# Attention's branch of a hybrid SSD and forgetting-attention layer: low pieces of T1 and T4 made with the differences and loaded, and T3's product in a bank of its own

## The chip, the cores and the metric

The kernel runs on one core of one Trainium2 chip. The metric is the device time of one execution in microseconds; of several runs the median is given. A profile shows one execution, instruction by instruction. Its span goes from the first to the last recorded instruction, and a little time lies around it.

## The reference

One layer of a hybrid decoder, 1024 tokens by 1024 channels, float32. Two branches start from the same normalised projection, and a gated merge, an output projection and a residual follow. Cut to what matters here:

```python
h = rmsnorm(x, pre_g)
z_ssm, xbc, dt, q, k, v, f, z_att, g_ssm, g_att = split(h @ w_in)
y_ssm = group_norm(ssd(conv(xbc), dt, a) * silu(z_ssm))          # Mamba-2 branch
s     = q @ k.T / 8 + F[t] - F[s]                                # 16 heads of 64, causal, F = cumsum(log sigmoid(f))
y_att = (softmax(s) @ v) * silu(z_att)                           # attention's branch
merged = sigmoid(g_ssm) * (y_ssm @ w_branch_ssm) + sigmoid(g_att) * (y_att @ w_branch_att)
x = x + rmsnorm(merged @ w_out, post_g)
```

## The kernel before, in words

**Large products.** Every projection is done with a Strassen-Winograd scheme over 2 x 2 blocks. A `Pair` (L320) takes two groups of 128 weight columns and gives two units of 128 output channels by 1024 tokens, in halves of 512 tokens. It needs seven products instead of eight. Each has a weight side (blocks a11, a12, a21, a22 or sums of them) and a data side, an operand made of four blocks of 128 rows by 512 columns (j = 0 to 3). The map `OPERAND` (L150) names the data side of each product: 1 uses b11, 2 b21, 6 -T2, 5 T1, 7 T3, 4 T4 and 3 -b22. The differences are T1 = b12 - b11, T2 = b22 - T1, T3 = T2 - b11 and T4 = T2 - b21 (`LESS`, L167).

**Three passes.** A float32 product is made of three passes in TensorE's fp32r form: each number is split into a high piece h (rounded by a ScalarE copy) and a low piece l (VectorE: the number less h), and the passes are h*h, h*l and l*h. So one product is 4 x 3 = 12 matmuls of 128 x 128 by 512 columns (`matmuls`, L386). The operand tiles in the profile are x0 (b11), x1 (b21), x2 (-b22), x3 (T1), x4 (-T2), x5 (T3) and x6 (T4), with h or l behind the number; a pair's split weights are `wop`.

**Where a product goes.** Products 1, 6, 7 and 4 of a pair add to one PSUM bank (`self.b`, shown as pb). After 1, 6 and 7 the running sum is copied to SBUF by ScalarE (`keep`, L399, line L402 of the profile), and TensorE can add the next product only after that copy. Products 5 and 3 add in another bank (pc). `give` (L405) forms a result from a bank and a kept sum on VectorE (L415 to L419), and the result of product 4 on ScalarE (L413), with the sign turned.

**The order.** `Stream` (L461) writes the order of all products by hand, pair after pair, two halves of six matmuls each. `half` (L535) issues one half, prepares the weights of the product three steps on (`prepare`: split on ScalarE L349 and VectorE L350, sums L355 on VectorE or GpSimd), fetches and splits operands of the next branch (`some`, L294), and runs one waiting chore from the list `chores`. The pairs after the projections are four of the Mamba branch (`ends[0:4]`, operands `ops_s`), four of attention's branch (`ends[4:8]`, operands `ops_a`) and four of the output projection (`ends[8:]`, operands `ops_w`). The first of attention's four, called a in the constructor, runs its products in the order 1, 5, 6 and then, when attention is done, 7, then product 1 of the next pair b, and 2, 4, 3.

**Attention** (L1327 to L1733) goes over eight head pairs hp and six groups g of query blocks each. One step m = 6 hp + g issues scores (L1476: TensorE, then VectorE's row maximum L1505 and ScalarE's exponential L1509), the weighted values of the step before (L1552), some halves of the stream, the transposes of the exponentials (L1511, L131) with their copies (L1546, L1548), and again some halves. Most instructions that belong to a step are pinned (`pin`): on each engine they keep the order of the program. TensorE's are all pinned. Unpinned instructions are placed by the framework when it builds the program.

**Differences of attention's branch.** A head pair hp gives block k = hp of y_att. For hp below 4 (L1580) the block's T1 is formed on VectorE from the outputs (`first`, L1585) and stored to DRAM by a chore through GpSimd's queue (`store`, L192, L193 of the profile). For hp = 4 to 6 `second` (L1592) makes T2 and T3, and `last` (L1607, L1609) makes T4, block j = hp - 4; they are stored likewise. For hp = 7 all are made in place and split without DRAM (`put`, L287, and `direct`, L282). `fetch` (L257) loads a block, raw, into the low tile, on SyncE's queue (SP, L263), and `split` (L265) makes its high piece on ScalarE (L275 or L278) and its low piece on VectorE (L276 or L279). For `ops_w` there is another way already: blocks named in `lows` have had their low piece made early and stored, so `fetch` loads both pieces (the raw block into the high tile) and `split` only rounds the high one.

**Small buffers.** `small` (L136) gives a tile of 128 x 512 floats from one pool of four buffers with the tag th. Gates and results of the stream (th), the fetched blocks of the differences (y, and th at L206), the softmax sums on their way (st, L1431, and rb, L1438) all take them. An instruction that fills a new one waits until the old one's last reader is done, which can be a store's landing.

Of the kernel before, what the change touches and what calls it, by code (L numbers as in the profile page):

```python
# [12 lines left out]
ALU = mybir.AluOpType  # L13
# [73 lines left out]
def hybrid_layer(ctx: ExitStack, tc, a, out):  # L87
# [71 lines left out]
    class Operands:  # L159
# [9 lines left out]
        def __init__(self, name, src, there=lambda k, h: True, order=lambda op: op, queue=nc.gpsimd):  # L169
            self.src, self.there, self.order, self.queue = src, there, order, queue  # L170
            self.copy = src
            self.tiles, self.left, self.made, self.at, self.step = {}, {}, set(), {}, 0
            self.lows = {}
            self.dram = {n: tc.dram_tile([KH, P, HALF], F32, name=f"{n}_{name}") for n in self.LESS}

        def __getitem__(self, name):
# [7 lines left out]
            return self.dram[name][j]  # L184

        def ready(self, name, j):
            if name in self.BLOCKS:
                r, h = self.BLOCKS[name]
                return self.there(KH * r + j, h)
            return (name, j) in self.made  # L190

        def store(self, name, j, t, cols=slice(0, HALF)):  # L192
            pin(self.queue.dma_start(self.dram[name][j][:, cols], t))  # L193
            if cols.stop == HALF:
                self.made.add((name, j))

        def differences(self, j, x, other, cols=slice(0, HALF), room=2, third=None):

# [65 lines left out]

        def split(self, name, j, raw=None):  # L265
            h, l = (t[:, j, :] for t in self.tiles[name])
            if name.strip("-") in self.lows:

                pin(nc.scalar.activation(h, h.bitcast(F32), AF.Copy, scale=-1.0 if name[0] == "-" else 1.0))
                self.left[name].remove(j)  # L270
                return
            if raw is None:
                raw = l.bitcast(F32)
            if name[0] == "-":
                pin(nc.scalar.activation(h, raw, AF.Copy, scale=-1.0))  # L275
                pin(nc.vector.scalar_tensor_tensor(l, raw, -1.0, h, ALU.mult, ALU.subtract))  # L276
            else:
                pin(nc.scalar.activation(h, raw, AF.Copy))  # L278
                pin(nc.vector.tensor_tensor(l, raw, h, ALU.subtract))  # L279
            self.left[name].remove(j)  # L280
# [39 lines left out]
    class Pair:  # L320
# [7 lines left out]
        def __init__(self, keys, handlers, ops=None, adds=nc.vector):  # L328
            self.keys, self.handlers = keys, handlers
            self.ops = xop if ops is None else ops  # L330
            self.adds = adds
            self.raw, self.op, self.prepared = {}, {}, set()
            self.s1, self.sums = None, 0

        def load(self, names):
            for n in names:
# [59 lines left out]
                        stop=k == KH - 1 and n == 2, skip_group_check=True,  # L396
                    )

        def keep(self, ps):  # L399
            s = wp.tile([P, HALF], F32, tag="s", bufs=3, name="s")  # L400
            with tc.high_priority():
                nc.scalar.activation(s, ps, AF.Copy)  # L402
            return s

        def give(self, unit, ch, ps, s=None, how=None):  # L405
            dst, post = self.handlers[unit][0:2]
            if s is None and hasattr(post, "direct"):
                post.direct(ch, ps)
                return
            d = dst(ch)  # L410
            with tc.high_priority():
                if s is None:
                    nc.scalar.activation(d, ps, AF.Copy, scale=-1.0)  # L413
                elif how == "sum":
                    nc.vector.tensor_tensor(d, ps, s, ALU.add)  # L415
                elif how == "less":
                    nc.vector.tensor_tensor(d, ps, s, ALU.subtract)
                else:
                    nc.vector.tensor_tensor(d, s, ps, ALU.subtract)  # L419
            post(ch)  # L420

        def begin(self, which, sums, early):
# [6 lines left out]
        def do(self, which):  # L429
            self.begin(which, self.sums, False)  # L430
            if which == 1:
                pool, tag = self.bank
                self.b = pool.tile([P, HALF], F32, tag=tag, bufs=1, name="pb")
                yield from self.matmuls(self.b, 1, "b11", True)
                self.k1 = self.keep(self.b)
            elif which == 2:
                pool, tag = self.other
                ps = pool.tile([P, HALF], F32, tag=tag, bufs=1, name="p" + tag)
                yield from self.matmuls(ps, 2, "b21", True)
                self.give(0, 0, ps, self.k1, "sum")  # L440
            elif which == 6:
                yield from self.matmuls(self.b, 6, "-t2", False)
                self.k2 = self.keep(self.b)
            elif which in (5, 7):
                if which == 5:
                    self.c = pj.tile([P, HALF], F32, tag="c", bufs=1, name="pc")
                    yield from self.matmuls(self.c, 5, "t1", True)
                else:
                    yield from self.matmuls(self.b, 7, "t3", False)
                    self.k7 = self.keep(self.b)  # L450
                self.sums += 1
                if self.sums == 2:
                    self.give(1, 1, self.c, self.k7, "less")
            elif which == 4:
                yield from self.matmuls(self.b, 4, "t4", False)
                self.give(1, 0, self.b)
            elif which == 3:
                yield from self.matmuls(self.c, 3, "-b22", False)
                self.give(0, 1, self.c, self.k2, "from")

    class Stream:  # L461
# [6 lines left out]
        def __init__(self, pairs, double, last):  # L468
            self.pairs = pairs
            for n, p in enumerate(pairs):  # L470
                p.bank, p.other = (pj, "be"[n % 2]), (pjx, "d") if n < double else (pj, "c")

                p.between = n < double or n >= last

# [6 lines left out]
                self.steps += [(p, 4), (p, 3)] if n + 1 < last else [(p, 3), (p, 4)]  # L481

            a, b, c, d, e, f, g, h = pairs[last:]
            self.steps += [(a, 5), (a, 6), (a, 7), (b, 1), (a, 2), (a, 4), (a, 3)]
            for p, nxt in ((b, c), (c, d), (d, e)):
                self.steps += [(p, 2), (p, 6), (p, 5), (p, 7), (nxt, 1), (p, 4), (p, 3)]
# [840 lines left out]
    with tc.tile_pool(name="att", bufs=1, reuse_waits="tile", side="right") as ap, tc.tile_pool(  # L1327
# [247 lines left out]
        def outputs(hp, h, zr):  # L1575
# [4 lines left out]
            if hp < KH:  # L1580
                if h == 0:
                    y = fetched("b12", hp)

                    def first():
                        pin(nc.vector.tensor_tensor(y, y, zr, ALU.subtract))  # L1585
# [207 lines left out]
```

## Time and profile before

| | us |
|---|---|
| median of 3 runs | 1278.0 (1276.09 to 1281.77) |
| the profiled execution | 1273.87 |
| its span | 1272.2 |
| TensorE busy (share of the span) | 1246.1 (98%) |
| VectorE busy | 1012.9 (80%) |
| ScalarE busy | 794.3 (62%) |
| GpSimd busy | 319.3 (25%) |
| granted TensorE clock, mean | 0.999 |

In the profile PE is TensorE's matmuls, PEld its weight loads, DVE VectorE, ACT ScalarE, POOL GpSimd and SP SyncE; SPq, ACTq and the like are instructions that only issue a DMA. A row of the timeline gives the start and the duration in us, the engine and the line of the kernel, the operation, output <- inputs, shape and count, and in brackets the idle time before it with what ended that. A matmul's record is longer than the step to the next one, since matmuls overlap. Attention's stage goes from about 670 to 1120 us; the rest of attention's branch and the output projection follow.

### The profile page before, as it was taken

The page shows a single profiled execution, that of the slowest core. Times are in us where ns is not written, and L with a number is a line of the kernel's source. Part 1 is how long each engine was busy: PE and PEld are TensorE (multiplying, and loading weights), DVE is VectorE, ACT ScalarE, POOL GpSimd, SP SyncE. Part 2 cuts the span into 40 slices and gives each one's busy share as a digit, 9 for nine tenths or more (in the row PEclk, how much of TensorE's full clock was granted, in tenths as well). Part 3 has the DMA queues.
Part 4 walks back from the last instruction along what each step waited for, and adds up shares of the span by engine and source line. Part 5 has one row for each costly group of instructions (what it writes and reads, how often), then busy time and mean ns, then how long its engine had stood idle before and what let it go on. Part 6 is the DMA issues. An engine that isn't in the chain of part 4 may idle for free.

```text
span 1272.2 us, 20822 instructions
## 1 busy us (share of the span) xinstructions
PE 1246.1 (98%) x6926; PEld 982.3 (77%) x6926; DVE 1012.9 (80%) x1994; ACT 794.3 (62%) x1737; POOL 319.3 (25%) x322
## 2 busy tenths in 40 slices
PE   5999999999999999999999999999999999999997
PEld 3678888888888888888887777777777777778886
DVE  7988886988888978997767676767789767886975
ACT  7745665556665765566555666666687666844753
POOL 4000440013400241115102124223112212356062
PEclk9999999999999999999999999999999999999999
DMA  8232452545436533744447576666687657766933
GB/s 300 69 120 76 146 162 88 191 152 182 138 101 215 175 127 117 219 146 140 142 149 252 162 228 212 217 214 218 232 286 263 224 184 249 249 221 199 364 110 105
DMA packets 152236, 233.56 MB, mean 184 GB/s; under 512 B 15201, under 2 KB 60737, under 8 KB 152129
## 3 DMA queue, kind: packets, MB, share of 16 engines
q1 hardware_dynamic: 136064, 196.08, 47.7%
q10 hardware_dynamic: 10560, 18.06, 3.8%
q0 software_dynamic: 5504, 18.09, 3.7%
q8 instruction: 54, 0.88, 0.3%
q14 instruction: 54, 0.43, 0.1%
HBM read 162.99 MB, written 72.34 MB: 185 GB/s over the span
## 4 chain that ended last, share of the span: by engine, by line
PE 86%; DMA 4%; DVE 4%; ACT 4%; issue 1%; SPq 0%; POOL 0%; DVEq 0%; ACTq 0%; POOLq 0%
PE pb L128 36%; PE pc L128 21%; PE pd L128 7%; PE av L128 5%; PE pt L131 5%; PE s L128 5%; PE yps L128 2%; PE st L128 1%; ACT ex L1509 1%; DMA xt<-in_x 1%; PE tr L131 1%; PE tr_v L131 1%; DMA v<-v_dram 1%; PE df L128 1%; DVE wop L350 1%
## 5 line engine op out<-in xcount | busy, mean ns | idle before, releaser
L350 DVE TENSOR_TENSOR wop<-sum,wop 128x512 fp32r<-128x512 f32 x180 | 140.2, 780 | 53.6 <-ACT wop L349 52.6
L349 ACT ACTIVATE wop<-sum 128x512 fp32r<-128x512 f32 x180 | 112.5, 626 | 109.0 <-DVE sum L355 52.4
L1509 ACT ACTIVATE ex<-ex,nm 128x512 f32<-128x512 f32 (+1 forms) x192 | 116.2, 606 | 71.9 <-DVE nm L1505 71.6
L402 ACT ACTIVATE s<-pb 128x512 f32<-128x512 f32 x144 | 85.3, 593 | 98.2 <-PE pb L128 96.2
L128 PE MATMUL pb<-x0h,wop 128*128 128x512 f32 x384 | 131.5, 399 | 0.0
L128 PE MATMUL pb<-x6h,wop 128*128 128x512 f32 x384 | 129.5, 395 | 1.3 <-ACT s L402 1.3
L128 PE MATMUL pb<-x5h,wop 128*128 128x512 f32 x384 | 130.1, 396 | 0.7 <-ACT s L402 0.7
L350 DVE TENSOR_TENSOR wop<-raw,wop 128x512 fp32r<-128x512 f32 x144 | 105.4, 733 | 31.8 <-ACT wop L349 31.5
L128 PE MATMUL pc<-x3h,wop 128*128 128x512 f32 x384 | 129.8, 396 | 0.5 <-DVE ot L419 0.4
L128 PE MATMUL pc<-x2h,wop 128*128 128x512 f32 x384 | 130.2, 397 | 0.0
L128 PE MATMUL pb<-x4h,wop 128*128 128x512 f32 x384 | 129.1, 395 | 0.0
L1505 DVE CUSTOM_DVE_ANT_0 ex<-s,fb 128x512 f32<-128x512 f32 (+1 forms) x192 | 96.8, 552 | 20.0 <-PE s L128 14.8
L349 ACT ACTIVATE wop<-raw 128x512 fp32r<-128x512 f32 x144 | 89.7, 623 | 14.7 <-PE pd L128 6.1
L128 PE MATMUL pd<-x1h,wop 128*128 128x512 f32 x288 | 96.3, 394 | 0.0
L128 PEld LDWEIGHTS pb<-x6h,wop 128*128 128x128 f32 x384 | 72.1, 188 | 18.6 <-issue 2.0
L128 PEld LDWEIGHTS pb<-x5h,wop 128*128 128x128 f32 x384 | 72.1, 188 | 18.4 <-issue 2.0
L128 PEld LDWEIGHTS pb<-x0h,wop 128*128 128x128 f32 x384 | 72.6, 189 | 17.6 <-issue 2.9
L128 PEld LDWEIGHTS pc<-x3h,wop 128*128 128x128 f32 x384 | 72.1, 188 | 17.7 <-issue 1.5
L128 PEld LDWEIGHTS pc<-x2h,wop 128*128 128x128 f32 x384 | 72.1, 188 | 17.4 <-issue 2.4
L128 PEld LDWEIGHTS pb<-x4h,wop 128*128 128x128 f32 x384 | 72.1, 188 | 16.7 <-issue 1.9
L211 POOL TENSOR_TENSOR wd<-wd 128x256 f32<-128x256 f32 x32 | 32.4, 1011 | 205.0 <-DMA wd<-in_wo 135.0
L131 PE MATMUL pt<-ident,ex 128*128 128x128 f32 x576 | 75.1, 273 | 2.0 <-ACT ex L1509 1.4
(318 smaller groups left out, 2993.6 us busy)
## 6 DMA issues: line engine op xcount, KB each, us to landing
raw<-in_wu SPq DMA_DIRECT2D x128, 256.0 KB
csb<-cs_dram SPq DMA_DIRECT2D x32, 256.0 KB
q<-q_dram SPq DMA_DIRECT2D x32, 256.0 KB
k<-k_dram SPq DMA_DIRECT2D x16, 512.0 KB
fb<-f_dram SPq DMA_DIRECT2D x16, 512.0 KB
rb<-st_dram SPq DMA_DIRECT2D x48, 128.0 KB
wd<-in_wo SPq DMA_DIRECT2D x40, 128.0 KB
xt<-in_x SPq DMA_DIRECT2D x8, 512.0 KB
```

The lines of the kernel that those rows point to most:

```text
L128: return tc.keep_in_program_order(nc.tensor.matmul(*args, **kw))
L131: return tc.keep_in_program_order(nc.tensor.transpose(out_, in_, idn))
L211: pin(nc.gpsimd.tensor_tensor(t[out_], t[a_], t[b_], ALU.subtract))
L349: nc.scalar.activation(op[:, 0], src, AF.Copy)
L350: nc.vector.tensor_tensor(op[:, 1], src, op[:, 0], ALU.subtract)
L402: nc.scalar.activation(s, ps, AF.Copy)
L1505: nc.vector.tensor_tensor_reduce(o, s[e][:, 0:w], fb[hp, h][:, e, 0:w], 1.0, 3.0e38, ALU.add, ALU.min, nm)
L1509: pin(nc.scalar.activation(o, o, AF.Exp, scale=-1.0, bias=nm, accum_out=hd.at(hd.sm, i, h, e)))
```

## The change

For T1 (all four blocks) and for the three blocks of T4 that go through DRAM, the low piece is now made when the difference is made, by a chore one half after the store: a rounding on ScalarE into a new th buffer, a subtraction on VectorE and a store through GpSimd's queue. At the end both pieces are loaded, and `split` only rounds the high one. A block counts as there (`made`) when its low piece has been issued. For pair a, product 7 (T3) goes to a bank of its own and starts it afresh; the sum kept after it is made by VectorE from that bank and the sum kept after product 6, and product 4's result, which adds in the new bank, is formed from it and that kept sum on VectorE.

The diff, cut to its core:

```diff
+            self.lows, self.late = {}, ()
...
         def ready(self, name, j):
-            if name in self.BLOCKS:
+            if name in self.BLOCKS and name not in self.late:
...
         def store(self, name, j, t, cols=slice(0, HALF)):
             pin(self.queue.dma_start(self.dram[name][j][:, cols], t))
-            if cols.stop == HALF:
+            if cols.stop == HALF and name not in self.late:
                 self.made.add((name, j))
+
+        def lower(self, name, j, t):
+            s = small()
+            pin(nc.scalar.activation(s.bitcast(F32R), t, AF.Copy, scale=-1.0 if name == "b22" else 1.0))
+            if name == "b22":
+                pin(nc.vector.scalar_tensor_tensor(s.bitcast(F32R), t, -1.0, s, ALU.mult, ALU.subtract))
+            else:
+                pin(nc.vector.tensor_tensor(s.bitcast(F32R), t, s, ALU.subtract))
+            pin(self.queue.dma_start(self.lows[name][j], s))
+            self.made.add((name, j))
...
         def split(self, name, j, raw=None):
-            if name.strip("-") in self.lows:
+            if raw is None and name.strip("-") in self.lows:
...
-        def keep(self, ps):
+        def another(self):
+            pool, tag = self.room
+            return pool.tile([P, HALF], F32, tag=tag, bufs=1, name="p" + tag)
+
+        def keep(self, ps, more=None):
             s = wp.tile([P, HALF], F32, tag="s", bufs=3, name="s")
             with tc.high_priority():
+                if more is not None:
+                    nc.vector.tensor_tensor(s, ps, more, ALU.add)
+                    return s
                 nc.scalar.activation(s, ps, AF.Copy)
...
-                else:
+                elif how == "from":
                     nc.vector.tensor_tensor(d, s, ps, ALU.subtract)
+                else:
+                    nc.vector.scalar_tensor_tensor(d, ps, -1.0, s, ALU.mult, ALU.subtract)
...
-                    yield from self.matmuls(self.b, 7, "t3", False)
-                    self.k7 = self.keep(self.b)
+                    if self.apart == 7:
+                        self.b = self.another()
+                    yield from self.matmuls(self.b, 7, "t3", self.apart == 7)
+                    self.k7 = self.keep(self.b, self.k2 if self.apart == 7 else None)
...
-                yield from self.matmuls(self.b, 4, "t4", False)
-                self.give(1, 0, self.b)
+                if self.apart == 4:
+                    self.b = self.another()
+                yield from self.matmuls(self.b, 4, "t4", self.apart == 4)
+                self.give(1, 0, self.b, {7: self.k2, 4: self.k7}.get(self.apart), "neither")
...
-                p.bank, p.other = (pj, "be"[n % 2]), (pjx, "d") if n < double else (pj, "c")
+                p.bank, p.other = (pj, "be"[(n + (n > last)) % 2]), (pjx, "d") if n < double else (pj, "c")
...
             a, b, c, d, e, f, g, h = pairs[last:]
+            a.apart, a.room = 7, (pj, "be"[(last + 1) % 2])
...
+    ops_a.late = ("t1", "t4")
+    ops_a.lows = {n: tc.dram_tile([KH, P, HALF], F32, name=f"{n}_low_a") for n in ops_a.late}
...
-                        stream.chores += [None, lambda: ops_a.store("t1", hp, y)]
+                        stream.chores += [None, lambda: ops_a.store("t1", hp, y), lambda: ops_a.lower("t1", hp, y)]
...
-                stream.chores += [None, lambda: ops_a.store("t4", j, x)]
+                stream.chores += [None, lambda: ops_a.store("t4", j, x), lambda: ops_a.lower("t4", j, x)]
```

The banks that the constructor gives to pairs after a are set again once attention is done (L1742), so the changed count there alters none of them.

More of the change, by code (lines that the diff above doesn't have):

```diff
@@ L172, in __init__ @@
             self.tiles, self.left, self.made, self.at, self.step = {}, {}, set(), {}, 0
-            self.lows = {}
+            self.lows, self.late = {}, ()
             self.dram = {n: tc.dram_tile([KH, P, HALF], F32, name=f"{n}_{name}") for n in self.LESS}
@@ L333, in __init__ @@
             self.s1, self.sums = None, 0
+            self.apart = None
         def load(self, names):
@@ L417, in give @@
                     nc.vector.tensor_tensor(d, ps, s, ALU.subtract)
+                elif how == "from":
+                    nc.vector.tensor_tensor(d, s, ps, ALU.subtract)
                 else:
-                    nc.vector.tensor_tensor(d, s, ps, ALU.subtract)
+                    nc.vector.scalar_tensor_tensor(d, ps, -1.0, s, ALU.mult, ALU.subtract)
             post(ch)
```

## The prediction

> **What bounds the kernel now.** I read the page's totals first, then the chain that ended last, then the table of stretches around the end of attention, then TensorE's own waits.
>
> ```profile
> span 1272.2 us, 20822 instructions
> PE 1246.1 (98%) x6926; PEld 982.3 (77%) x6926; DVE 1012.9 (80%) x1994; ACT 794.3 (62%) x1737; POOL 319.3 (25%) x322
> ...
> PE 86%; DMA 4%; DVE 4%; ACT 4%; issue 1%; SPq 0%; POOL 0%; DVEq 0%; ACTq 0%; POOLq 0%
> ```
>
> TensorE is busy for 98% of the span and carries 86% of the chain, so a change can only win time in which TensorE waits, or lose by making it wait. The stretches (columns: PE, PEld, DVE, ACT, POOL busy with counts, clock, DMA share, GB/s) show where the change acts.
>
> ```profile
> 1090.00:1095.00 5.00, 5.00 (x32) 4.39 (x31) 4.08 (x12) 5.00 (x13) 0.68 (x1) 1.00 1.05 372
> 1095.00:1100.00 5.00, 5.00 (x40) 3.26 (x39) 5.00 (x13) 2.89 (x7) 2.10 (x2) 1.00 1.04 385
> ...
> 1110.00:1115.00 5.00, 4.65 (x24) 3.34 (x23) 4.63 (x11) 5.00 (x15) 0.00 (x0) 1.00 0.60 197
> 1115.00:1120.00 5.00, 4.76 (x25) 3.17 (x23) 4.99 (x10) 2.73 (x6) 0.54 (x1) 1.00 0.54 139
> 1120.00:1125.00 5.00, 4.55 (x20) 3.79 (x21) 4.78 (x8) 3.98 (x8) 2.97 (x1) 1.00 1.02 363
> 1125.00:1130.00 5.00, 5.00 (x24) 4.14 (x23) 4.83 (x7) 2.53 (x5) 3.58 (x4) 1.00 0.23 45
> ```
>
> From 1110 to 1125 VectorE is busy 14.40 of 15 us and TensorE 13.96: for this one stretch VectorE is the tighter engine. The clock is 1.00 throughout and plays no part. TensorE's instructions there, and the two links of the chain that hold them up:
>
> ```profile
> 1112.14 0.47 PE L128 MATMUL pc<-x3h,wop 128*128 128x512 f32 x1
> 1112.96 0.50 PE L128 MATMUL pc<-x3l,wop 128*128 128x512 f32 x1 [0.35 <-DVE x3l L279]
> ...
> 1115.95 0.87 PE L128 MATMUL av<-p,v 128*64 128x256 f32 x8
> ...
> 1119.37 0.39 PE L128 MATMUL pb<-x4h,wop 128*128 128x512 f32 x1
> 1120.45 0.50 PE L128 MATMUL pb<-x5h,wop 128*128 128x512 f32 x1 [0.69 <-ACT s L402]
> ...
> 1123.30 0.39 PE L128 MATMUL pb<-x0h,wop 128*128 128x512 f32 x1
> ```
>
> ```profile
> 1112.22 0.69 DVE x3l L279
> ...
> 1119.80 0.61 ACT s L402
> ```
>
> Here pc<-x3 is T1's product (5) of the first attention pair, pb<-x4 the product of T2 (6), pb<-x5 that of T3 (7). T3's twelve matmuls take 2.85 us (1120.45 to 1123.30). T1's take 3.81 (1112.14 to 1115.95): they wait for low pieces that VectorE is still making, and lose 3.81 - 2.85 = 0.96. Between T2's last matmul and T3's first lie 1.08 us, where matmuls of one product follow each other after about 0.23 (2.85 / 12): 0.85 is lost while ScalarE copies the bank that T3's product goes on adding to. That is 1.81 us in all, and the marked idle time (0.35 and 0.69) shows only part of it, since a matmul's record outlasts the step to the next.
>
> [...]
>
> **The change, part by part.** The operations that it moves and adds have these rows (count, then busy us and mean ns):
>
> ```profile
> L279 DVE TENSOR_TENSOR x3l<-x3l,x3h 128x512 fp32r<-128x512 f32 x12 | 8.0, 685 | 1.2 <-ACT x3h L278 1.2
> L278 ACT ACTIVATE x3h<-x3l 128x512 fp32r<-128x512 f32 x12 | 6.9, 616 | 0.0
> L193 POOL DMA_DIRECT2D t_a<-y x7 | 3.8, 544 | 18.4 <-DVE y L1585 18.0 <-issue 0.4
> L415 DVE TENSOR_TENSOR th<-pd,s 128x512 f32<-128x512 f32 x20 | 13.7, 683 | 0.9 <-PE pd L128 0.9
> ```
>
> *Removed at the end:* seven subtractions (four blocks of T1, three of T4), 7 x 0.685 = 4.8 us of VectorE between 1109 and 1130. T1's product then waits only for ScalarE's roundings, which stay as they are. Gain: 0.96, from the wait that ends last there. T4's three subtractions stand under no TensorE wait, so they give no time of their own.
>
> *T3's product in another bank:* the wait of 0.85 goes. What is late next is T3's last low piece, and VectorE, relieved of 4.8 us, should reach that earlier. The copy after the product turns into an addition (0.683 in place of about 0.6, VectorE for ScalarE), and T4's result is formed by VectorE instead of ScalarE: 1.4 us of VectorE added, still 3.4 less than before. I cost these at nothing, since T1's difference is not needed by TensorE; with that cover gone they cost 1.4.
>
> *Added in attention:* seven times a rounding (0.616), a subtraction (0.685) and a store (0.544 to issue on POOL's queue, 256 KB). All three are pinned. From below they cost nothing (work added before TensorE's next need frees nothing, so it cannot gain); from above, all of ScalarE's and VectorE's time on TensorE's path, 7 x 1.3 = 9.1. Behind the subtraction, in order on VectorE, stands the next group's row maximum (L1505), for it ScalarE's exponentials wait, and for those TensorE's transposes. The store on POOL has the masks behind it. The first place:
>
> ```profile
> 756.65 0.52 SPq L206 DMA_DIRECT2D th<-ys_dram  x1
> 758.40 0.25 ACT L1431 ACTIVATE st<-pt 8x128 f32<-8x128 f32 x1
> 759.20 0.33 ACTq L630 DMA_DIRECT2D gs_dram<-th  x1
> 763.29 0.71 ACT L1509 ACTIVATE ex<-ex,nm 128x512 f32<-128x512 f32 x1
> ```
>
> ```profile
> 755.01 0.68 DVE L1585 TENSOR_TENSOR y<-y,zr 128x512 f32<-128x512 f32 x1
> 760.42 0.69 DVE L1505 CUSTOM_DVE_ANT_0 ex<-s,fb 128x512 f32<-128x512 f32 x1 [0.86 <-PE s L128]
> 764.18 0.69 DVE L419 TENSOR_TENSOR th<-s,pc 128x512 f32<-128x512 f32 x1 [0.76 <-DMA st_dram<-st]
> ```
>
> ```profile
> 764.67 1.91 PE L131 MATMUL pt<-ident,ex 128*128 128x128 f32 x16
> ```
>
> The low piece needs a "th" buffer, of which there are four, and here four are taken: y itself, the fetched block of 756.65, st, and the gate whose store is issued at 759.20. The gate's buffer comes free when that store lands:
>
> ```profile
> DMA to landing us min/median/max: 2.3/3.8/7.2
> ```
>
> So (from the landings of the "th" tile) at about 763. Rounding and subtraction then end at 764.3, and the row maximum starts 3.9 us late. The fourth exponential ended at 764.0, and the last four of the sixteen transposes, the first to need it, would come some 1.2 us after 764.67, so 1.9 of the 3.9 are covered and 2.0 are lost; with a landing after 2.3 us, 0.5. Elsewhere I read the same queues more favourably: a buffer is free, or the next row maximum starts later by less than the 1.9 that the exponentials' lead covers here. I take 1.0 for all seven, near the low bound, because one place of seven looks uncovered.
>
> [...]
>
> *Loads at the end:* seven more of 256 KB on SP's queue. T1's four fall where the DMA engines are full: 1.05 MB at the 372 to 385 GB/s of the table is 2.8 us, and four more issues 1.7.
>
> ```profile
> 1095.21 1.37 SPq L263 DMA_DIRECT2D x3l<-t_a  x3
> ```
>
> ```profile
> 1106.66 1.13 ACT L278 ACTIVATE x3h<-x3l 128x512 fp32r<-128x512 f32 x2
> ```
>
> The last T1 load is issued before 1096.6; with the median 3.8 to land it is there at 1100.4, and in the new kernel at 1104.9, still ahead of the first rounding at 1106.66. More loads cannot bring a gain, so the low end is nothing, and I take it; if the lead of 1.8 us is used up (a landing of 7.2, the slowest, would do), ScalarE stands still up to about 1.6 us, with the last exponentials of attention behind it.
>
> **The sum.** -0.96 - 0.85 + 1.0 = -0.8 us on a profiled execution of 1273.9 us (span 1272.2 and 1.7 around it): 1273.1. That execution lies 4.1 us below the median of the runs shown, 1278.0 (1276.09 to 1281.77), so for the median I say **1277.2**. About 0.5%, 6.4 us, is what a measurement of this kernel tells from no change.
>
> **The rivals.**
> *No buffer (slower).* The one mechanism is the four "th" buffers: the pinned rounding stands on ScalarE until some store lands, and softmax stands behind it. For it speaks the row at 764.18, where VectorE already waits for such a buffer. Against it: such waits are rare in attention, and most places have a free buffer by my reading. At 2.0 a place, seven places make 14 - 1.8 = +12: 1290. At half of them, +5: 1283. It decides from the point where the places together lose over 1.8 us; over 0.5% from 8.2. Chance 0.22, a little over half of it beyond 0.5%.
>
> *The gain is handed on to GpSimd.* Once TensorE runs 1.8 us earlier, the next pair's sums must be ready earlier too:
>
> ```profile
> 1138.58 0.63 ACT L349 ACTIVATE wop<-sum 128x512 fp32r<-128x512 f32 x1 [5.80 <-POOL sum L355]
> ...
> 1142.34 0.39 PE L128 MATMUL pb<-x5h,wop 128*128 128x512 f32 x1
> ```
>
> ScalarE waited 5.8 us for GpSimd's sum, and the weights made of it serve at 1142.34. Rounding and low piece (0.63 and 1.10 here) end near 1140.35, 2.0 ahead. If GpSimd's sum does not move, this lead just covers 1.8; if the added loads make it 2 us later, the gain is lost: +1.0 - 1.8 + 1.8, so 1279. For it: the lead is that small. Against: the sum itself follows merges that come earlier too. Chance 0.20.
>
> *It frees VectorE for more.* VectorE is the tight engine from 1110 to 1125, and a net 3.4 us leave it; if all of that were on the path, -3.4 + 1.0: 1275.6. Against: the trace names only 1.81 as waits. Chance 0.14.
>
> *Nothing is moved.* The rounding of T1 stays, so if it and not the subtraction held T1's product, 0.96 would remain and the kernel would be at 1278.2. The row at 1112.96 names the subtraction; chance within the second rival's.
>
> **How the numbers follow.** The forecast has 0.44. Range: from 1273 (1275.6 less the 1.9 by which the lowest run lies under the median, rounded out) to 1285 (the upper bound 9.1 - 1.8 above 1278). Beyond it remain the full no-buffer case and odd reorderings, under 0.2. No named wait reaches 6.4 us, so faster by over 0.5%: 0.04, for an order of instructions drawn up anew that happens to suit. Slower by over 0.5%: 0.13. Within: 0.83.
>
> **What would show it.** After: T1's product takes about 2.85 us with no wait for a low piece; T2's and T3's products follow without a gap; x3l and x6l have loads and, but for one block of T4, no subtraction. The seven low pieces appear on VectorE in attention, and TensorE's transposes wait no more than about 1 us in all for exponentials behind them. The forecast is wrong if the place near 759 repeats itself, seen as ScalarE idle until a store lands and transposes waiting; or if TensorE is ahead at 1123 but not at 1145.

## The result and the profile after

The changed kernel took 1287.93 us, the median of 6 runs (1286.78 to 1293.13), beside 1277.7 us for 6 runs of the kernel before (1276.09 to 1281.77): a ratio of 1.0083, 95% interval 1.006 to 1.0105. That is about 10 us slower, where 1277.2 with a range up to 1285 had been forecast. The profiled execution of the changed kernel (called after) was the longest of the six, 1293.13 us, and that of before, 1273.87, lies below all six of its runs. So the two traces lie 19.2 us apart (spans 1291.4 and 1272.2), twice the distance of the medians. Places and causes are read from the traces, and so are sizes by place; what a whole change costs is taken from the medians.

The page's totals and the chain that ended last, after:

```profile
span 1291.4 us, 20855 instructions
...
PE 1255.6 (97%) x6926; PEld 986.9 (76%) x6926; DVE 1016.3 (79%) x1996; ACT 796.1 (62%) x1742; POOL 320.3 (25%) x329
...
PE 72%; DMA 10%; DVE 8%; ACT 5%; issue 3%; SPq 1%; POOL 0%; ACTq 0%; DVEq 0%; POOLq 0%
```

TensorE does the same 6926 matmuls, but its share of the chain fell from 86% to 72%, and DMA, VectorE and ScalarE took it. First the end of attention, at which the change was aimed: T1's product (pc<-x3) and the passage from T2's product to T3's (pb<-x4 to pe<-x5), then T3's end:

```profile
1131.11 0.48 PE L128 MATMUL pc<-x3h,wop 128*128 128x512 f32 x1
...
1134.02 0.87 PE L128 MATMUL av<-p,v 128*64 128x256 f32 x8
...
1137.49 0.39 PE L128 MATMUL pb<-x4h,wop 128*128 128x512 f32 x1
1137.72 0.39 PE L128 MATMUL pe<-x5h,wop 128*128 128x512 f32 x1
```

T1's product now takes 2.91 us (3.81 before), and 0.23 lie between the last matmul of T2 and the first of T3 (1.08 before). The two gains of the forecast, 0.96 and 0.85, are there as 0.90 and 0.85. They don't last. The timeline of all engines just behind them:

```profile
1132.67 0.43 SPq L274 DMA_DIRECT2D x6h<-t_a  x1
1134.33 0.27 ACTq L1460 DMA_DIRECT2D st_dram<-st  x1
...
1139.87 1.66 SPq L1466 DMA_DIRECT2D rb<-st_dram  x2
...
1144.05 0.69 DVE L1491 TENSOR_TENSOR zr<-o,rb 128x512 f32<-128x512 f32 x1 [4.34 <-DMA rb<-st_dram]
...
1146.46 0.68 DVE L290 TENSOR_TENSOR x1l<-zr,x1h 128x512 fp32r<-128x512 f32 x1
...
1147.20 0.50 PE L128 MATMUL pd<-x1l,wop 128*128 128x512 f32 x1 [1.24 <-DVE x1l L290]
```

Attention's last sums go through DRAM. Their store is issued at 1134.33, and the load that waits for it can start only at 1139.87, 5.5 us later. VectorE stands for 4.34 us, the last block's low piece (x1l) is late, and TensorE waits for it. In before the same steps took 1.3 us; there three loads of T4 stand just ahead of them on SP's queue, here six, and behind these two loads of weights that in before come later:

```profile
1114.84 0.27 ACTq L1432 DMA_DIRECT2D st_dram<-st  x1
```

```profile
1116.12 1.10 SPq L1438 DMA_DIRECT2D rb<-st_dram  x2
```

The experiments below bear this out. From store to load it takes 1.3 to 1.5 us in the seven traces with three loads of T4 (before, e1, e3, e6, e9, e10, e13), and 3.8 to 6.4 us in eight of the nine with six. In the ninth, e5, the store comes 3.1 us behind the last of the six, and it takes 1.8.

Now attention. The waits from 668 to 1135 us (who waited for whom: us in total, times, longest):

```profile
DVE th L204 <- ACT th L200: 8.2, 5, 5.3
...
PE pt L131 <- ACT ex L1537: 7.2, 13, 2.2
...
ACT th L200 <- DMA st_dram<-st: 6.6, 3, 4.5
```

L200 is the rounding of the low piece, L204 its subtraction. Of the 6.6 us, 4.5 are at the first place of T1 and 2.1 at two places of T4. TensorE's transposes (L131) waited 7.2 us for the exponentials (L1537) behind them; in before the same wait was:

```profile
PE pt L131 <- ACT ex L1509: 1.4, 3, 0.9
```

The first place, in order of time:

```profile
759.63 0.29 ACTq L1460 DMA_DIRECT2D st_dram<-st  x1
...
765.08 0.63 ACT L200 ACTIVATE th<-y 128x512 fp32r<-128x512 f32 x1 [4.49 <-DMA st_dram<-st]
...
765.80 0.69 DVE L204 TENSOR_TENSOR th<-y,th 128x512 fp32r<-128x512 f32 x1 [5.29 <-ACT th L200]
766.41 0.68 DVE L1533 CUSTOM_DVE_ANT_0 ex<-s,fb 128x512 f32<-128x512 f32 x1
...
768.01 0.71 PE L131 MATMUL pt<-ident,ex 128*128 128x128 f32 x3 [2.24 <-ACT ex L1537]
```

The rounding gets the buffer of the sums, whose store lands 5.4 us after its issue. The row maximum (L1533), which in before started at 760.42, starts at 766.41. The transposes that in before ran from 764.67 without a stop begin at 768.01 and come in pieces. And TensorE then runs at a lower clock (columns: TensorE's busy time, the other engines', then the granted clock, DMA share, GB/s):

```profile
764.00:769.00 5.00, 2.48 (x12) 1.48 (x10) 3.20 (x10) 2.49 (x6) 1.81 (x2) 1.00 0.40 153
769.00:774.00 5.00, 4.57 (x19) 3.61 (x19) 4.78 (x14) 3.84 (x10) 2.26 (x3) 0.66 0.82 296
...
930.00:935.00 5.00, 3.39 (x18) 2.32 (x16) 3.68 (x12) 3.00 (x7) 1.02 (x2) 1.00 0.77 201
935.00:940.00 5.00, 3.96 (x17) 3.05 (x16) 3.67 (x9) 4.15 (x11) 1.36 (x2) 0.72 0.71 271
...
1120.00:1125.00 5.00, 2.90 (x25) 1.77 (x25) 0.84 (x2) 3.37 (x9) 2.92 (x3) 1.00 0.71 244
1125.00:1130.00 5.00, 5.00 (x23) 3.51 (x20) 3.25 (x12) 2.25 (x10) 0.56 (x1) 0.66 0.30 97
```

Three times a stretch of five microseconds at a clock of 0.66 to 0.72 follows one with 1.6 to 2.5 us of idle time. A clock of 0.66 over five microseconds is (1 - 0.66) x 5 = 1.7 us of lost work, so I estimate some 5 us for the three, on top of the idle time.

To see where time goes I matched the same matmuls in order and took the difference of their starts in the two traces. The change of this lag over a stretch is what the stretch lost (in us; stretches by the times of before):

| stretch | what is in it | after |
|---|---|---|
| 763 to 935 | T1's four low pieces | +12.8 |
| 935 to 1095 | T4's three low pieces | +1.3 |
| 1095 to 1111 | T1 is loaded | +3.9 |
| 1111 to 1124 | products 5, 6 and 7 of the first pair | -1.8 |
| 1124 to 1140 | the next products | +2.3 |

Up to 763 the lag is 1.0, behind 1140 it no longer grows. T4's third rounding, at 1100.71 in after, is at about 1086 by the times of before, so what is lost from 1095 on lies behind all seven low pieces.

### The profile page after: what moved, and what is told of

It is laid out like the page before. It is cut to its first block, busy times and chain, and to the rows that moved or that the text cites. A ratio compares the mean times of both kernels' runs of the same rounds, so it can differ in the third digit from the quotient of the medians.

```text
span 1291.4 us, 20855 instructions
## 1 busy us (share of the span) xinstructions
PE 1255.6 (97%) x6926; PEld 986.9 (76%) x6926; DVE 1016.3 (79%) x1996; ACT 796.1 (62%) x1742; POOL 320.3 (25%) x329
## 4 chain that ended last, share of the span: by engine, by line
PE 72%; DMA 10%; DVE 8%; ACT 5%; issue 3%; SPq 1%; POOL 0%; ACTq 0%; DVEq 0%; POOLq 0%
PE pb L128 31%; PE pc L128 17%; PE pd L128 6%; PE pt L131 4%; PE av L128 4%; PE s L128 4%; PE yps L128 2%; DMA st_dram<-st 2%; ACT ex L1537 2%; DVE wop L362 2%; DMA raw<-in_wu 1%; DMA rb<-st_dram 1%; PE st L128 1%; DMA xt<-in_x 1%; PE tr L131 1%
## 5 line engine op out<-in xcount | busy, mean ns | idle before, releaser
L1537 ACT ACTIVATE ex<-ex,nm 128x512 f32<-128x512 f32 (+1 forms) x192 | 116.1, 606 | 76.9 <-DVE nm L1533 76.0
L128 PE MATMUL pb<-x5h,wop 128*128 128x512 f32 x376 | 127.3, 395 | 0.0
L1533 DVE CUSTOM_DVE_ANT_0 ex<-s,fb 128x512 f32<-128x512 f32 (+1 forms) x192 | 96.7, 552 | 19.1 <-PE s L128 13.4
L131 PE MATMUL pt<-ident,ex 128*128 128x128 f32 x576 | 79.0, 277 | 9.1 <-ACT ex L1537 7.2
```

The costliest lines, as they stand in the source:

```text
L128: return tc.keep_in_program_order(nc.tensor.matmul(*args, **kw))
L131: return tc.keep_in_program_order(nc.tensor.transpose(out_, in_, idn))
L1533: nc.vector.tensor_tensor_reduce(o, s[e][:, 0:w], fb[hp, h][:, e, 0:w], 1.0, 3.0e38, ALU.add, ALU.min, nm)
L1537: pin(nc.scalar.activation(o, o, AF.Exp, scale=-1.0, bias=nm, accum_out=hd.at(hd.sm, i, h, e)))
```

## Experiments

The theory at first: the low piece's rounding waits, in ScalarE's fixed order, for one of four "th" buffers, and everything of softmax stands behind it (**buffer**). Rivals: the seven roundings and subtractions themselves (**work**), and seven more stores and loads (**traffic**). Diffs are against the changed kernel unless stated; the ratio is against the kernel before on the same chip, with its 95% interval.

### One half of the change alone

e1, no low pieces, T3's bank as changed:

```diff
-    ops_a.late = ("t1", "t4")
+    ops_a.late = ()
```

(the two `lower` chores go too).

> T3's product in the other bank alone, no low piece made in the attention's branch. Buffer theory (the low piece's buffer is what costs): no episode before 1100 us, the tail gains up to 0.85 us, time 1276.8 to 1277.8. Rival, the other bank or the longer VectorE work at the end costs: 1280 or more, with the wait at the end of the profile.

Measured 1278.44 us, ratio 1.0017 (1.0005 to 1.0029). By the lag no place before 1095 lost anything; the passage to T3 came 0.95 us earlier, and then:

```profile
1125.75 0.68 DVE L419 TENSOR_TENSOR s<-pe,s 128x512 f32<-128x512 f32 x1
...
1132.16 0.68 DVE L290 TENSOR_TENSOR x6l<-x6l,x6h 128x512 fp32r<-128x512 f32 x1
...
1132.89 0.50 PE L128 MATMUL pe<-x6l,wop 128*128 128x512 f32 x1 [1.69 <-DVE x6l L290]
```

The new addition (L419) stands on VectorE ahead of T4's last low pieces, and product 4 waits 1.69 us for one. The bank alone costs about 2 us (0.0017 x 1276): above the buffer theory's range, with the rival's mechanism, if less than its 1280.

e2, the low pieces without the bank:

```diff
-            a.apart, a.room = 7, (pj, "be"[(last + 1) % 2])
+            a.apart = None
```

> The low pieces as in the change, T3's product left in its old bank. Buffer theory: the same stalls of the transposes (some 5 us of waits for the exponentials and a granted clock near 0.5 behind each), 1287 to 1290. Rival, the bank and the low pieces cost together only: 1280 to 1283.

1291.23 us, ratio 1.0118 (1.0093 to 1.0143), with the same stalls (transposes wait 7.2 us for exponentials). The loss is the low pieces'.

### Buffer, work and traffic apart

e3, a buffer is taken at the same place, with 8 of 512 columns worked on and stored to a tensor of its own:

```diff
+            pin(nc.scalar.activation(s[:, 0:8].bitcast(F32R), t[:, 0:8], AF.Copy, scale=-1.0 if name == "b22" else 1.0))
...
+                pin(nc.vector.tensor_tensor(s[:, 0:8].bitcast(F32R), t[:, 0:8], s[:, 0:8], ALU.subtract))
+            pin(self.queue.dma_start(self.scratch[name][j][:, 0:8], s[:, 0:8]))
```

> Bank of the change; the low piece takes its buffer at the same place, but only 8 of its 512 columns are rounded, subtracted and stored, into a tensor that nobody reads; at the end T1 and T4 are split as before. Buffer theory: the wait for a buffer stays, so the time stays at 1284 to 1290. Rival, the work of 7 roundings and subtractions in the order of the two engines: 1277 to 1279. Rival, the traffic of seven stores and seven loads: 1277 to 1278.

1282.33 us, ratio 1.0064 (1.0039 to 1.0089). The wait is the same to the digit, and the transposes are late without the work:

```profile
764.89 0.21 ACT L200 ACTIVATE th<-y 128x8 fp32r<-128x8 f32 x1 [4.49 <-DMA st_dram<-st]
...
766.86 0.71 PE L131 MATMUL pt<-ident,ex 128*128 128x128 f32 x3 [1.28 <-ACT ex L1536]
```

It lies below the 1.0083 of the whole change, but the intervals overlap; the lags further down tell the two apart (3.6 and 12.8 us at T1's places). Neither theory's range holds it: the buffer theory's 1284 to 1290 was too high, the rivals' 1277 to 1279 too low.

e9, the whole rounding and subtraction, written into the idle buffer of exponentials and not stored:

```diff
-            pin(self.queue.dma_start(self.lows[name][j], s))
-            self.made.add((name, j))
...
+                        stream.chores += [None, lambda: ops_a.store("t1", hp, y), lambda: ops_a.lower("t1", hp, y, ex[:, 0, 0, :])]
...
+                stream.chores += [None, lambda: ops_a.store("t4", j, x), lambda: ops_a.lower("t4", j, x, ex[:, 0, 0, :])]
```

> The bank of the change, and at each of the seven places the whole rounding and the whole subtraction in the same order, but into the idle buffer of exponentials: no buffer of the ring, no wait for a store, no store, no loads; at the end T1 and T4 are split as before. Buffer theory: as with the bank alone, ratio 1.001 to 1.003, 1278 to 1281. Rival, the work: 1285 to 1287. If wait and work add up against one slack: below both, and no place with over 0.5 us of idle PE.

1284.42 us, ratio 1.0055 (1.0038 to 1.0072): between theory and rival. The third reading fails too, since TensorE idles 1.26 us at one place. That place, near 867, shows how 1.3 us of work become more:

```profile
866.00 0.63 ACT L652 ACTIVATE th<-th 128x512 f32<-128x512 f32 x1 [0.57 <-DVE th L433]
867.04 0.63 ACT L199 ACTIVATE ex<-y 128x512 fp32r<-128x512 f32 x1 [0.41 <-ACT th L652]
867.70 0.69 DVE L203 TENSOR_TENSOR ex<-y,ex 128x512 fp32r<-128x512 f32 x1 [0.41 <-ACT ex L199]
868.54 0.69 DVE L1529 CUSTOM_DVE_ANT_0 ex<-s,fb 128x512 f32<-128x512 f32 x1
...
873.26 0.98 PE L131 MATMUL pt<-ident,ex 128*128 128x128 f32 x7 [1.26 <-ACT ex L1533]
```

The row maximum on VectorE (L1529) now stands behind a subtraction that stands behind ScalarE's rounding, and that behind a gate: the pair ties VectorE's order to ScalarE's. The same row maximum in before:

```profile
865.72 0.68 DVE L1505 CUSTOM_DVE_ANT_0 ex<-s,fb 128x512 f32<-128x512 f32 x1
```

It is 2.8 us later now, 2.0 without the 0.8 by which this trace lies behind there, for 1.3 us of work.

e10, only one more store, of the difference itself:

```diff
+            pin(self.queue.dma_start(self.scratch[name][j], t))
```

> The bank of the change, and at each of the seven places one more whole store of the difference itself, into a tensor that nobody reads: traffic and GpSimd's seven issues alone, without rounding, subtraction or another buffer; at the end as before. Buffer theory and work: 1278 to 1280, as with the bank alone. Rival, the traffic: 1283 or more, with stores of the sums that land later.

1283.56 us, ratio 1.0052 (1.0037 to 1.0066), what the rival asked for (1283 or more). But the trace shows that traffic is not alone here: T1's difference lies in a "th" buffer too, and the second store holds it longer:

```profile
759.62 0.54 POOL L200 DMA_DIRECT2D t_low_a<-y  x1
...
767.66 0.69 DVE L432 TENSOR_TENSOR th<-s,pc 128x512 f32<-128x512 f32 x1 [1.69 <-DMA t_low_a<-y]
```

So each of the three partial doses costs 4 to 6 us more than the bank alone (0.0035 to 0.0047 of 1276, give or take 3 us by the intervals), and the whole 8.4 us (0.0066). By the medians the doses together cost more than the whole, and "the buffer alone" falls, since e9 costs 4.9 us without taking a buffer.

### Other places and other buffers

e4, each `lower` chore two half units later, behind the next step's transposes (here and in e12 T4's chore is edited alike):

```diff
-                        stream.chores += [None, lambda: ops_a.store("t1", hp, y), lambda: ops_a.lower("t1", hp, y)]
+                        stream.chores += [None, lambda: ops_a.store("t1", hp, y), None, None, lambda: ops_a.lower("t1", hp, y)]
```

> The whole change, but each low piece is made two half units of the stream later, behind the next step's transposes. Buffer theory: the rounding no longer stands behind a just issued store of the sums and ahead of the row maxima, 1276 to 1281 and fewer than 3 us of transposes waiting for exponentials. Rival, the work: 1285 to 1289, since the same instructions stand there. Rival, the traffic: 1286 to 1289.

1284.53 us, ratio 1.0074 (1.0048 to 1.0099): against 1.0083 no gain that the intervals show. At the second place, which has no wait in after, there is one now, for another landing, and GpSimd's mask and the row maximum stand behind it:

```profile
820.77 0.33 ACTq L656 DMA_DIRECT2D ga_dram<-th  x1
...
825.32 0.63 ACT L200 ACTIVATE th<-y 128x512 fp32r<-128x512 f32 x1 [2.27 <-DMA ga_dram<-th]
...
829.78 0.68 DVE L1533 CUSTOM_DVE_ANT_0 ex<-s,fb 128x512 f32<-128x512 f32 x1
...
831.37 1.48 PE L131 MATMUL pt<-ident,ex 128*128 128x128 f32 x8 [1.54 <-ACT ex L1537]
```

e12, store and low piece in one chore, ahead of this step's transposes:

```diff
+                        stream.chores += [None, lambda: (ops_a.store("t1", hp, y), ops_a.lower("t1", hp, y))]
```

> The whole change, but the low piece is made in the half unit of its own store, ahead of this step's transposes and of the buffer of the sums: its rounding no longer waits for the store of the sums. Buffer theory as stated for that one store: 1277 to 1281. Rival, any taker of a fifth buffer waits: the sums' own buffer waits in its place, 1284 to 1289 with the same stalls.

1295.3 us, ratio 1.0134 (1.0103 to 1.0165): the rival's mechanism, and worse than its 1289. Now the sums' own buffer waited 4.0 us for the store of T1's difference.

e11, both instructions on GpSimd:

```diff
+            pin(nc.gpsimd.tensor_copy(s.bitcast(F32R), t))
+                pin(nc.gpsimd.tensor_tensor(s.bitcast(F32R), t, s, ALU.subtract))
```

> The whole change, but rounding and subtraction of the low pieces are put on GpSimd, so that the wait for a buffer stands in its order and not in ScalarE's and VectorE's. Buffer theory: the row maxima are no longer behind the wait, 1276 to 1280, some transposes still late where GpSimd's mask comes behind it. Rival, the ring itself: other users of the ring wait, 1283 to 1288.

1286.7 us, ratio 1.0069 (1.0042 to 1.0096): the rival again. GpSimd waited 18.5 us for landings before its roundings. At the first place a result of the stream (L438) on VectorE then waited 2.6 us for GpSimd's subtraction, and TensorE 2.6 us for a copy (L1574) that stands behind this result on VectorE.

e7, the rounded copy s in the idle buffer of exponentials (`ex[:, 0, 0, :]`, as in e9), the low piece over the difference:

```diff
+                pin(nc.vector.tensor_tensor(t.bitcast(F32R), t, s, ALU.subtract))
+            pin(self.queue.dma_start(self.lows[name][j], t))
```

> The whole change, but the rounded copy is put into the buffer of exponentials, which is idle at that place, and the low piece written over the difference itself: no buffer of the ring is taken, and the subtraction waits for the difference's own store, issued some 8 us earlier. Buffer theory: 1276 to 1281. Rivals, the work or the traffic: 1285 to 1289.

1303.17 us, ratio 1.0186 (1.0162 to 1.0211), the worst of the runs that keep four buffers of split weights. Here the subtraction waited for the store of its own difference (6.3 us at T1's places, 1.5 at T4's): a new wait ahead of the row maxima, so it says nothing of the old one.

e5, a buffer of its own, for which the ring of split weights gives room, and e6, the kernel before with that ring:

```diff
-            op = wp.tile([P, 2, KH, P], F32R, tag="wop", bufs=4, name="wop")
+            op = wp.tile([P, 2, KH, P], F32R, tag="wop", bufs=3, name="wop")
...
+            return ap.tile([P, HALF], F32, tag="lw", bufs=1, name="lw")
```

> The whole change, the low piece in a buffer of its own at the same place in ScalarE's and VectorE's order; the room for it comes from the ring of split weights, 3 buffers in place of 4, so it is read against e6_before_wop3. Buffer theory: within 3 us of e6, and no rounding that waits for a store. Rival, the work in the two engines' order: 7 to 10 us above e6. Rival, the traffic: 9 to 11 us above e6.

> Control: the kernel before with 3 buffers of split weights in place of 4. It tells what that ring costs alone; no theory bears on it. If the ring had slack 1276 to 1280, else some tens of us more.

1395.11 and 1385.89 us. The ring had no slack: it costs 108 us, the transposes wait 42 us for exponentials, and every added instruction counts. The 9.2 us between the two, with no rounding that waits for a store, are close to 7 x 1.3 of work; but these kernels wait far more everywhere, so this settles nothing for the change itself. A fifth "th" buffer without such a loan was not tried; it would be the direct trial of the buffer theory.

### T1 or T4

e8, T4's three low pieces with the bank; e14, the same without the bank (as e2); e13, T1's four with the bank. The other operand's `lower` chore goes.

```diff
-    ops_a.late = ("t1", "t4")
+    ops_a.late = ("t4",)
```

(in e13 `("t1",)`).

> The change with T4's three low pieces alone, T1 as before. From the trace of the changed kernel, the three places of T4 lost some 1 us near 982, 0.4 near 1050 and up to 3.6 near 1104: buffer theory 1278 to 1283. Rival, the work, alike at every place: a share of 3 in 7, 1281 to 1282 with transposes late at each of the three. If the pieces cost only where four buffers are out: below 1280.

> The change with T1's four low pieces alone, T4 as before, the bank as in the change. Ring theory (T1's difference and its low piece both hold buffers of the ring while the other branch's differences use it; T4's difference has a buffer of its own): ratio 1.007 to 1.010, 1285 to 1289. Rival, every place alike: four parts in seven, ratio 1.005, 1282 to 1284.

> T4's three low pieces alone, without the other bank. Ring theory: no loss at T4's places, ratio 0.999 to 1.002, 1276 to 1280, and the subtractions that leave the end give nothing by themselves. Rival, every place alike: three parts in seven, ratio 1.004 and above, 1281 to 1283.

e8: 1279.23 us, ratio 1.0011 (0.9996 to 1.0026). e14: 1279.39 us, ratio 1.0021 (1.001 to 1.0032). e13: 1289.99 us, ratio 1.0098 (1.0079 to 1.0118). T1's four pieces cost as much as all seven, and T4's three with the bank can't be told from no change. Without the bank they cost 2.7 us (0.0021 x 1276), just clear of zero. The rule "every place alike" falls. The rounding's rows in e13, then in e8:

```profile
L200 ACT ACTIVATE th<-y x4: 617/632/632, 764.7 to 929.0; 128x512 fp32r<-128x512 f32 x4
...
  DMA st_dram<-st: 4.2, 1
  DMA ga_dram<-th: 1.5, 1
```

```profile
L200 ACT ACTIVATE th<-x x3: 631/632/635, 978.2 to 1087.5; 128x512 fp32r<-128x512 f32 x3
...
  DMA st_dram<-st: 0.5, 1
```

In e13 the rounding waits 5.7 us for landings at T1's places, 4.2 of them at the first, and in e8 0.5 at T4's. But in after T4's first two places waited as well:

```profile
930.63 0.63 ACT L200 ACTIVATE th<-y 128x512 fp32r<-128x512 f32 x1 [1.56 <-DMA ga_dram<-th]
991.94 0.63 ACT L200 ACTIVATE th<-x 128x512 fp32r<-128x512 f32 x1 [1.00 <-DMA st_dram<-st]
...
1047.47 0.64 ACT L200 ACTIVATE th<-x 128x512 fp32r<-128x512 f32 x1 [1.10 <-DMA st_dram<-st]
```

The last of T1's places (930.63) lost 4.8 us behind a wait of 1.56, and T4's three together 1.3 behind waits of 1.00 and 1.10. So the wait by itself does not say what a place loses. The lag by stretch, for the runs that matter (us):

| stretch | after | T1 only e13 | T4 only e8 | bank e1 | thin e3 | work e9 | traffic e10 |
|---|---|---|---|---|---|---|---|
| 763 to 935 | 12.8 | 11.3 | 0.1 | -0.6 | 3.6 | 3.9 | 1.4 |
| 935 to 1095 | 1.3 | -0.2 | 0.8 | -0.1 | -0.1 | 0.1 | 0.7 |
| 1095 to 1111 | 3.9 | 4.3 | 3.6 | 0.4 | 2.1 | 0.8 | 0.1 |
| 1111 to 1124 | -1.8 | -1.8 | -0.7 | 0.2 | -1.4 | -1.0 | -0.5 |
| 1124 to 1140 | 2.3 | 2.0 | 0.0 | 2.0 | 2.0 | 2.0 | 2.0 |

The first row by T1's four places (us lost, each line from one trace; the last line is what the rounding waited for a landing in after):

| place (time in after) | 765 | 817 | 873 | 930 |
|---|---|---|---|---|
| after | 5.2 | 0.9 | 2.0 | 4.8 |
| T1 only e13 | 4.0 | 0.2 | 2.4 | 4.6 |
| thin e3: wait, hardly any work | 3.0 | -0.6 | 0.3 | 1.0 |
| work e9: no wait | -0.3 | -0.4 | 2.5 | 2.2 |
| traffic e10 | 1.9 | -0.5 | 0.1 | 0.0 |
| wait in after | 4.49 | 0 | 0 | 1.56 |

So the four places do not lose for one reason: the first loses by the wait for a buffer, the third by the work in the two engines' order, the last by both, and the second hardly at all. At T1's places whole and doses differ by 12.8 - (3.6 + 3.9 + 1.4) = 3.9 us, the bank's -0.6 aside. Two stretches of lower clock lie there in after, some 3.4 us by the estimate above, none in e9 and e10 (mean clock 0.999, as in before), and none in e3 at the first place (1.00 from 764 to 779); that is most of the difference. In the medians it is the other way round. The traces of e9 and e10 are of their shortest runs (1281.3 and 1280.17), that of after of its longest, so how exactly the parts combine stays open. The stretch from 1095 varies from 0.1 to 4.3 with and without T1's loads. In after its stall is a "th" buffer again, held by a store issued at 1114.67, just behind T1's eight loads; what tips it elsewhere was not settled.

## Why the prediction was wrong

**The step that failed is the price of the low pieces in attention: 1.0 us for seven places.** By the medians it is 8.4 us (0.0066 x 1276, the bank's 2.2 aside), and by e13 and e8 it belongs to T1's four low pieces. The forecast looked for the loss at the first place alone and took the others for covered. The runs showed two places that lose by a wait for a store's landing, two that lose by the 1.3 us of work in ScalarE's and VectorE's order, one of them in both lists, and in after a clock of 0.66 to 0.72 behind three of the stalls. The sign of being wrong that the forecast named came true: the place near 759 repeats itself, and TensorE, 1.8 us ahead by 1124, has lost that by 1140. Point by point:

*T1's product, -0.96, and T3's bank, -0.85:* right, 0.90 and 0.85 in the trace of after.

*What is late next:* wrong. Forecast was T3's last low piece; it was the last sums' way through DRAM in after, and T4's low pieces on VectorE in e1. The forecast costed the addition on VectorE at nothing because of T1's difference. That is not what covers it: in e13, where T1's subtractions are gone, the stretch from 1124 loses 2.0 as in e1, and in e8, where T4's are gone, 0.0. The bound of 1.4 given for lost cover was near.

*Loads at the end, 0:* wrong. The loads themselves came in time, but a small store behind them came late: the sums took 5.5 us from store to load instead of 1.3, and the stretch from 1124 handed back the gain. In e8 and e2, where one of the two gains is missing, and in e14, where both are, the sums were as late (4.5 to 5.3) and that stretch lost nothing. So it is a price of the gain: TensorE must be early to stand there. The forecast asked whether the loads arrive, and not who stands behind them.

*The first place near 759:* read rightly in kind, and too cheaply. The four holders were named, and the row maximum was put 3.9 us late; it was 6.0 by the two traces' own times, 5.0 without the lag of 1.0 that was there already. The buffer that the rounding got did not come free with the gate's store "at about 763" but with that of the sums near 765. The loss was put at 0.5 to 2.0; it was 5.2, of which 2.94 is TensorE's idle time and about 1.7 the clock.

*The other places, "a free buffer by my reading":* partly right as a reading, wrong as a price. At T1's second and third place the rounding waited for no landing, but the third lost 2.0 all the same, and e9 loses 2.5 there by the work alone. At the fourth it waited 1.56 us and the place lost 4.8. At T4's first two places it waited 1.00 and 1.10 us, and T4's three lost 1.3 together. The places were not read one by one. By the code, y, the other branch's block, st and a gate are out together at T1's places, and T4's difference has a tile of its own; that this makes T1's places dearer is argued, not shown.

*The clock, "plays no part":* right for before (mean 0.999), wrong for after, where it was 0.66 to 0.72 in the five microseconds behind three stalls. No rival carried it.

*The rivals:* the one without a buffer named the wait and gave 1290 for seven places, 1283 for half; it was held at 0.22. Its place by place price is not right either, and the wait is not the whole: e3, wait without work, is 6.0 us above the bank alone, e9, work without wait, 4.9. GpSimd's sum taking the gain was not seen. That VectorE is freed for more was not seen.

*The subtractions, 0.685 each:* right for T1's four, which took 0.67 to 0.69. Of T4's three two took 0.69, and one, at 1101.38, 1.00 us, while GpSimd's sum (L367) runs from 1100.22 to 1101.83. It is worth 0.3 us here; what made this one longer was not shown.

## What to carry to other kernels

When a small piece of work is put into a fixed order ahead of the critical engine's next input, go through its places one by one. List for each who holds its buffer, which landing sets it free, and how much slack the engines behind it have: here one place lost by the wait, one by the work, one by both. In a ring that is shared with stores look for the latest landing: here one came 5.4 us after its issue, and moving the taker within the ring moved the wait to another one (2.27 us for a gate's store in e4, 4.0 us of the sums' own buffer in e12). Ask of added transfers not only whether they arrive in time but which small transfer comes late behind them. And split an experiment by operand: two kinds of block with the same instructions cost some 10 us (e13 above the bank alone, 0.0081 x 1276) and nothing (e8).

## What the runs showed of the hardware

In after a stall of TensorE cost more than its idle time: the first place lost 5.2 us, of which 2.94 were idle. After three stretches with 1.6 to 2.5 us idle in five, the granted clock was 0.66 to 0.72 in the next five, in a finer slice 0.50:

```profile
770.00:772.00 2.00, 1.76 (x8) 1.47 (x9) 1.95 (x5) 1.76 (x5) 1.35 (x2) 0.50 0.91 308
```

The clock record kept with the trace gives the drops themselves. In after there are three before the program's end, at 769.99, 937.24 and 1124.98 us, each 3.413 us long at 0.50; half of that, 1.7 us, is my estimate of what one costs if TensorE has work throughout. The distances of their starts, 167.25 and 187.74 us, are 49 and 55 times that length. No values but 0.50 and 1.00 stand in the records of before and after. In e2 the clock of the ten microseconds from 769 on comes to as much as one such drop, (0.23 + 0.11) x 5 = 1.7 us:

```profile
769.00:774.00 5.00, 4.16 (x19) 3.23 (x19) 4.97 (x14) 4.42 (x12) 2.53 (x4) 0.77 0.86 299
774.00:779.00 5.00, 5.00 (x37) 2.99 (x37) 3.08 (x11) 2.71 (x7) 0.00 (x0) 0.89 0.35 126
```

What brings a drop about was not settled. In e1 five microseconds with 3.31 busy, the 1.69 us gap among them, were followed by a clock of 1.00:

```profile
1130.00:1135.00 5.00, 3.31 (x15) 2.43 (x14) 5.00 (x7) 1.73 (x3) 2.44 (x3) 1.00 0.48 159
1135.00:1140.00 5.00, 5.00 (x24) 4.14 (x23) 4.96 (x6) 0.32 (x2) 5.00 (x4) 1.00 0.50 154
```

In e3 five microseconds with 1.82 us idle, from 764 on, were followed by a clock of 1.00, and in e10 five with 1.65, all in one gap, from 770 on. In e4 TensorE waited 1.54 us in one gap, up to 831.37, and the mean clock of that trace is 0.999, as in before. In after the drop at 937.24 came behind 1.61 us idle from 930 to 935 and no gap over 1.32 us, and in e2 the five microseconds from 764 on, ahead of the lower clock, had 1.59 idle. So neither the longest gap nor the idle time in five microseconds tells the cases apart. The longest gap between matmul rows in attention in after was 2.24 us, ahead of the first drop.
